# Matmul with batch normalisation: the weight's last two blocks loaded and computed one at a time, the second chunk by halves of rows

## The chip, the cores and the metric

The kernel runs on one core of a Trainium2 chip. The metric is the device time of one execution in microseconds (us), measured without a profiler; the profile beside it is one further execution, recorded. TensorE multiplies, VectorE (DVE), ScalarE (ACT) and GpSimd (POOL) compute, SyncE (SP) and GpSimd issue DMA transfers.

## The reference

```python
# x: (16, 512, 1024), weight: (1024, 768), gamma and beta: (768,), all float32
y = np.matmul(x, weight)
mean = np.mean(y, axis=(0, 1), keepdims=True)
var = np.var(y, axis=(0, 1), keepdims=True)
y_norm = (y - mean) / np.sqrt(var + eps)
return (gamma * y_norm + beta).astype(np.float32)
```

So an 8192 x 1024 matrix is multiplied by a 1024 x 768 one, and each of the 768 columns of the product is normalised by its own mean and variance over all 8192 rows. No output can be written before all 8192 rows of its column are multiplied.

## The kernel before

The 8192 rows are cut into C = 16 chunks of 512 (`CH`), each of two quarters of 256 rows (`QR`); the 1024 inner positions into four blocks (`JW`) of 256; the 768 columns into six groups of 128. x and w are converted to bf16 by the loading DMA. DVE transposes each piece of x into `xT_sb`[...].

Two forms of matmul are used. For column groups 0 and 1 (`GA`) of chunks 0 to 13 the *row form* puts rows of x on the partitions of the result, two blocks of 128 rows in one PSUM bank:

```python
def mm_rows(c, ts, jws, slot):
    def emit(eng):
        if jws[0] == 0:
            y_ps = psum.tile([P, CH], f32, tag="b")
            slot.tile = y_ps
        y_ps = slot.tile.rearrange("p (s n) -> p s n", n=NA)
        for s, t in enumerate(ts):
            for jw in jws:
                for e in range(2):
                    seq(nc.tensor.matmul(
                        y_ps[:, s], x_slot[c].tile[:, jw, t * P:(t + 1) * P, e],
                        w_sb[:, jw, e, 0:NA], ...))
```

For column groups 2 to 5, and for groups 0 and 1 of the last two chunks (`ga_unit`), the *column form* puts the columns on the partitions:

```python
for jw in jws:
    for e in range(2):
        seq(nc.tensor.matmul(
            y_ps, w_sb[:, jw, e, nt * P:(nt + 1) * P],
            x_slot[c].tile[:, jw, q0 * QR:q1 * QR, e], ...))
```

So one row unit is 16 matmuls of 256, one column unit 8 matmuls of 512. Each result bank is read by DVE or ACT for its statistics and copied to bf16 by ACT. There are eight PSUM banks. Row units are squared by ACT, their values added up by DVE and their squares by GpSimd or DVE. After chunk 15 the sums are merged, spread to all partitions by four small matmuls (`a_ps`), and the first outputs are written; the column units of groups 2 to 5 for chunks 4 to 15 fill TensorE's time meanwhile and afterwards.

The kernel is written as tasks with priorities, durations and dependences. A function `arrange` sorts them, as the kernel is built, into one fixed order for each engine[...]. At most eight loads of GpSimd's queue are under way: a load waits for the landing of the load eight before it. One load task issues four DMAs, each for 32 partitions:

```python
def load_w(jw, jw1):
    def emit(eng):
        rows = weight.rearrange("(i jw c e) n -> i c jw (e n)", i=4, jw=JW, e=2)
        dst = w_sb.rearrange("p jw e n -> p jw (e n)")
        for i in range(4):
            seq(nc.gpsimd.dma_start(dst[32 * i:32 * i + 32, jw:jw1], rows[i, :, jw:jw1]))
    return emit

order = [("x", 0), ("w", 0, 1), ("x", 1), ("w", 1, 2), ("w", 2, 4)]
order += [("x", q) for q in range(2, SHORT * QPC)] + [("c", c) for c in range(SHORT, C - 1)]
order += [("p", M - CH, CH - P), ("p", M - P, P)]
```

`("x", q)` is a quarter of x, `("c", c)` a whole chunk, `("p", row, rows)` a part of the last chunk (384 rows, then 128). Chunk 0 is computed as the blocks of w come, chunk 1 by units:

```python
part(0, 1, [0])
...                       # eight idle matmuls that keep TensorE going
part(1, 2, [0])
part(0, 2, [1])
for h in range(2):
    rows_unit(0, [2 * h, 2 * h + 1], [2, 3])
for nt in range(GA, NT):
    col_unit(nt, 0, [2, 3])
...
for c in range(1, RC):
    for ts in ([0, 1], [2, 3]):
        rows_unit(c, ts)
    if c < EARLY:
        for nt in range(GA, NT):
            for jws in halves:
                col_unit(nt, c, jws)
```

Of the kernel before, what the change touches and what calls it, by code (L numbers as in the profile page):

```python
# [227 lines left out]
def kernel(  # L228
# [34 lines left out]
    GY = 2  # L263
    PAD = 36
    HELD = 1
# [60 lines left out]
    msq = singles.tile([P, GA], f32)  # L326
    gst = singles.tile([P, GA, 3 + 12 * (C - RC)], f32)
    seq(nc.vector.memset(gst, float(RC * CH)))
# [20 lines left out]
    def dve(occ):  # L349
        return {"DVE": (occ, occ + 0.09)}  # L350
# [57 lines left out]
    for c in range(C):  # L408
        x_slot[c] = Slot(xts)
    order = [("x", 0), ("w", 0, 1), ("x", 1), ("w", 1, 2), ("w", 2, 4)]  # L410
    order += [("x", q) for q in range(2, SHORT * QPC)] + [("c", c) for c in range(SHORT, C - 1)]
# [3 lines left out]
    for kind, n, *n1 in order:  # L415
# [29 lines left out]
        if rows % QR:  # L445
            t0 = rows // QR * QR // 32
            m1 = m0 + 32 * t0
            c, q = divmod(m1 // QR, QPC)
            x_ready["tile", m1 // P] = task(
                -1000 + t, dve(0.63), turn_x(slot, x_slot[c], m0, t0, 0, JW, False, P),  # L450
                [load, x_ready[c, 0, JW]], uses=[slot, x_slot[c]])
            x_ready[c, q, JW] = x_ready[c, q, JW // 2] = x_ready["tile", m1 // P]
# [3 lines left out]

    def mm_rows(c, ts, jws, slot):
        def emit(eng):
            if jws[0] == 0:
                y_ps = psum.tile([P, CH], f32, tag="b")  # L460
                slot.tile = y_ps
            y_ps = slot.tile.rearrange("p (s n) -> p s n", n=NA)
            for s, t in enumerate(ts):
                for jw in jws:
                    for e in range(2):
                        seq(nc.tensor.matmul(  # L466
                            y_ps[:, s], x_slot[c].tile[:, jw, t * P:(t + 1) * P, e],
                            w_sb[:, jw, e, 0:NA],
                            start=(s == 0 and jw == 0 and e == 0),
                            stop=(jw == JW - 1 and e == 1),  # L470
                            skip_group_check=True,
                        ))
        return emit
# [56 lines left out]

    def rows_unit(c, ts, jws=range(JW)):
        key = "row", c, ts[0]
        slot = bank_of.setdefault(key, None) or Slot(banks)
        bank_of[key] = slot
        kw = {"takes": [slot], "uses": [x_slot[c]]} if jws[0] == 0 else {"uses": [slot, x_slot[c]]}
        h = ts[0] * P // QR
        t = pe_task(0.873 * len(ts) * len(jws) / JW, mm_rows(c, ts, list(jws), slot),
                    waits(jws, c, h, h + 1), key, **kw)
        if jws[-1] == JW - 1:
            rows_stats(c, ts, slot, t)  # L540
        return t
# [21 lines left out]
    def rows_stats(c, ts, slot, t):  # L563
# [11 lines left out]
        def add_rows(eng):  # L575
            seq(nc.vector.tensor_add(sum1, slot.tile[:, 0:n], sum1))  # L576

# [118 lines left out]
    part(0, 2, [1])  # L696
    for h in range(2):
        rows_unit(0, [2 * h, 2 * h + 1], [2, 3])
    for nt in range(GA, NT):
        col_unit(nt, 0, [2, 3])  # L700

# [8 lines left out]

    def more(h):
        def emit(eng):
            seq(nc.gpsimd.tensor_add(tot[:, 1], tot[:, 1], sum3[:, h * NA:(h + 1) * NA]))
        return emit

    ga_half = {}

    def ga_unit(nt, c, q, cols=QR):
        slot = Slot(banks)
        at = 3 + 6 * (2 * (c - RC) + q)  # L720

        def emit(eng):
            y_ps = psum.tile([P, CH], f32, tag="b")
            slot.tile = y_ps
            for jw in range(JW):
                for e in range(2):
                    seq(nc.tensor.matmul(  # L727
                        y_ps[:, 0:cols], w_sb[:, jw, e, nt * P:(nt + 1) * P],
                        x_slot[c].tile[:, jw, q * QR:q * QR + cols, e],
                        start=(jw == 0 and e == 0), stop=(jw == JW - 1 and e == 1),  # L730
                    ))
# [4 lines left out]
        def keep(eng):  # L736
            if "y" not in y_row[c].__dict__:
                y_sb = ypool.tile([P, GA, CH], bf16, tag="y")
                y_row[c].y = y_sb
            seq(nc.scalar.copy(y_row[c].y[:, nt, q * QR:q * QR + cols], slot.tile[:, 0:cols]))  # L740

        t = pe_task(1.808 * cols / CH + 0.01, emit, waits(range(JW), c, q, (q * QR + cols) // QR), takes=[slot],
                    uses=[x_slot[c]])
        late = 40 if c == C - 1 else -3.0
# [3 lines left out]
                 uses=[slot] + ([y_row[c]] if mine else []), takes=[] if mine else [y_row[c]])  # L748
        ga_half[nt, c, q] = b, k

    for c in range(1, RC):
        for ts in ([0, 1], [2, 3]):
# [5 lines left out]
    ends = [row_end[k] for k in row_end]  # L758
    U = clock[0] - 30.0
    for c in range(RC, C):  # L760
        for q in range(QPC):
            for nt in range(GA):
                ga_unit(nt, c, q)
    merges.append(task(U, dve(0.36), merge(0), [k[1] for k in ends], True))
    merges.append(task(U, pool(0.65), merge(1), [k[2] for k in ends]))
    for h in range(2):
        merges.append(task(U, pool(0.65), more(h), merges[1:]))

# [113 lines left out]

    ng = task(S - 30.0, dve(0.1), negate_gamma, [affine], True)

# [309 lines left out]
```

## Time and profile before

| | before |
|---|---|
| time, median of 3 runs | 212.51 us (212.29 to 212.88) |
| span of the profiled execution | 211.0 us |
| busy: TensorE, DVE, ACT, GpSimd | 193.6, 142.4, 127.2, 101.6 us |
| TensorE on the chain that ended last | 82% |
| loaded x and w on GpSimd's queue | 18.36 MB (as bf16) |

The profile divides the span into 40 slices of 5.27 us and shows for each the busy tenths of every engine and of the 16 DMA engines. Matmuls are pipelined and their ends are modelled, so a busy TensorE is not one at its peak; where it starts late after a wait is exact. In a line of a timeline the first number is the start in us from the span's start, the second the duration; `L466` is the line of the program (466: row form, 494: column form, 405: transpose by DVE, 384: load of x, 375: load of w, 727: `ga_unit`), and the bracket at the end tells how long the engine was idle before and what ended that.

### The profile page before, as it was taken

How to read it: one execution, taken by the hardware profiler on the slowest of the kernel's cores; microseconds unless marked ns; L12 is line 12 of the kernel's file. 1: busy time of each engine (PE TensorE's matmuls, PEld its weight loads, DVE VectorE, ACT ScalarE, POOL GpSimd, SP SyncE). 2: the span in 40 equal slices, each digit the busy share in tenths (PEclk: the TensorE clock that was granted, in tenths of full speed). 3: DMA queues.
4: the chain of work that ended last, by engine and by line, in shares of the span. 5: the costliest groups of instructions: out<-in, count | busy, mean ns of one | idle time of the engine just before them, and what ended most of it. 6: DMA issues, size and time to landing. Idle time of an engine off the chain costs nothing.

```text
span 211.0 us, 3457 instructions
## 1 busy us (share of the span) xinstructions
PE 193.6 (92%) x1218; PEld 114.1 (54%) x1234; DVE 142.4 (67%) x233; ACT 127.2 (60%) x233; POOL 101.6 (48%) x126
## 2 busy tenths in 40 slices
PE   7986999999999999999999999999999999996900
PEld 2363564647488888777854544444444455544600
DVE  4220887778759999978979898765963486247800
ACT  2000573435325666758279997999846687955940
POOL 7885967677529999997108985540000000000000
PEclk9999999999999999999999999999999999999985
DMA  5999999999999999999004999998999999994997
GB/s 51 167 179 184 186 196 196 196 197 196 191 193 197 194 198 196 196 196 185 11 2 149 339 385 322 263 355 236 317 253 254 324 322 332 345 347 143 320 347 227
DMA packets 95135, 47.92 MB, mean 227 GB/s; under 512 B 20880, under 2 KB 94608, under 8 KB 95120
## 3 DMA queue, kind: packets, MB, share of 16 engines
q0 software_dynamic: 34688, 18.36, 63.9%
q1 hardware_dynamic: 60432, 29.37, 49.1%
q8 instruction: 9, 0.15, 0.3%
q14 instruction: 6, 0.05, 0.1%
HBM read 36.71 MB, written 25.17 MB: 293 GB/s over the span
## 4 chain that ended last, share of the span: by engine, by line
PE 82%; DMA 6%; ACT 3%; POOL 3%; issue 1%; DVE 1%; ACTq 0%; POOLq 0%
PE y_ps L494 51%; PE y_ps L466 22%; PE y_ps L727 3%; DMA w_sb<-in_weight_dram 3%; ACT o_sb L1143 3%; DMA ring<-in_x_dram 2%; PE o_ps L961 2%; POOL w_sb L375 2%; POOL ring L384 1%; PE y_ps L665 1%; PE o_ps L991 1%; ACTq L1189 0%; PE a_ps L826 0%; PE tot_ps L781 0%; DVE fin L672 0%
## 5 line engine op out<-in xcount | busy, mean ns | idle before, releaser
L494 PE MATMUL y_ps<-xT_sb,w_sb 128*128 128x512 bf16 (+1 forms) x497 | 118.2, 383 | 0.7
L494 PEld LDWEIGHTS <-w_sb 128*128 128x128 bf16 x512 | 48.9, 96 | 62.1
L384 POOL DMA_DIRECT2D ring<-in_x_dram x76 | 47.5, 629 | 14.1 <-DMA ring<-in_x_dram 6.2
L466 PE MATMUL y_ps<-w_sb,xT_sb 128*128 128x256 bf16 x448 | 50.6, 273 | 2.7 <-DMA w_sb<-in_weight_dram 2.2
L466 PEld LDWEIGHTS <-xT_sb 128*128 128x128 bf16 x448 | 43.5, 98 | 10.5 <-issue 2.4
L625 DVE BATCH_NORM_STATS2 stats<-y_ps 128x6 f32<-128x512 f32 x46 | 31.8, 693 | 25.7 <-PE y_ps L494 25.5
L629 ACT CAST y_sb<-y_ps 128x512 bf16<-128x512 f32 x51 | 29.5, 586 | 26.0 <-DVE stats L625 17.6
L405 DVE STREAM_TRANSPOSE xT_sb<-ring 128x1024 f32<-128x1024 f32 (+1 forms) x35 | 38.2, 1128 | 10.2 <-DMA ring<-in_x_dram 10.2
L573 ACT ACTIVATE sq_sb<-y_ps 128x512 f32<-128x512 f32 x28 | 16.1, 598 | 27.3 <-PE y_ps L466 26.1
L859 POOL TENSOR_TENSOR ring<-ring,sum 128x1024 f32<-128x1024 f32 (+1 forms) x11 | 22.7, 2091 | 17.5 <-ACT sum L830 10.2
L580 POOL TENSOR_TENSOR sum<-sum,sq_sb 128x512 f32<-128x512 f32 x18 | 23.0, 1280 | 7.1 <-ACT sq_sb L573 6.6
L576 DVE TENSOR_TENSOR sum<-y_ps,sum 128x512 f32<-128x512 f32 x28 | 18.9, 676 | 10.7 <-ACT sq_sb L573 9.6
L586 ACT CAST y_sb<-y_ps 128x512 bf16<-128x512 f32 x28 | 16.2, 585 | 10.0 <-DVE sum L576 9.9
L961 PE MATMUL o_ps<-ident,y_sb 128*128 128x128 bf16 x128 | 17.1, 220 | 1.8 <-DVE y_sb L1130 1.6
L854 DVE TENSOR_TENSOR ring<-y_sb,a_ps 128x1024 f32<-128x1024 bf16 (+1 forms) x16 | 16.7, 1078 | 1.5 <-PE a_ps L826 0.8
L1057 ACT CAST ring<-ring 128x1024 f32<-128x1024 bf16 x16 | 16.7, 1048 | 0.8 <-DMA ring<-y_sb 0.8
L510 PE MATMUL idle_ps<-idle_sb 128*128 128x512 bf16 x37 | 10.8, 460 | 1.2 <-DVE idle_sb L309 1.2
L961 PEld LDWEIGHTS <-y_sb 128*128 128x128 bf16 x128 | 9.3, 97 | 3.8 <-DVE y_sb L1130 2.0
L940 ACT ACTIVATE y_sb<-y_sb,shift,scale 128x1024 bf16<-128x1024 bf16 x8 | 9.8, 1244 | 0.0
L634 ACT ACTIVATE y_sb<-y_ps 128x512 bf16<-128x512 f32 x12 | 7.1, 594 | 3.8 <-PE y_ps L494 3.8
L1035 ACT CAST ring<-o_ps 128x1024 f32<-128x1024 bf16 x8 | 8.1, 1024 | 0.3 <-DMA out_dram<-ring 0.3
L510 PEld LDWEIGHTS <-idle_sb 128*128 128x128 bf16 x38 | 4.2, 114 | 7.1 <-issue 3.3
(87 smaller groups left out, 113.1 us busy)
## 6 DMA issues: line engine op xcount, KB each, us to landing
out_dram<-ring SPq DMA_DIRECT2D x38, 512.0 KB, 3.9
ring<-in_x_dram POOLq DMA_DIRECT2D x52, 256.0 KB, 9.1
out_dram<-o_sb SPq DMA_DIRECT2D x6, 512.0 KB, 5.2
ring<-in_x_dram POOLq DMA_DIRECT2D x16, 128.0 KB, 5.4
out_dram<-ring SPq DMA_DIRECT2D x4, 256.0 KB, 2.1
w_sb<-in_weight_dram POOLq DMA_DIRECT2D x8, 96.0 KB, 4.8
w_sb<-in_weight_dram POOLq DMA_DIRECT2D x4, 192.0 KB, 6.3
ring<-in_x_dram POOLq DMA_DIRECT2D x4, 192.0 KB, 8.0
```

The source lines that it names most:

```text
L384: seq(nc.gpsimd.dma_start(x_bf[32 * i:32 * i + 32], src[:, :, KQ * i:KQ * (i + 1)]))
L405: seq(nc.vector.transpose(dst, src[:, :, jw0:jw1]))
L466: seq(nc.tensor.matmul(y_ps[:, s], x_slot[c].tile[:, jw, t * P:(t + 1) * P, e], w_sb[:, jw, e, 0:NA], start=(s == 0 and jw == 0 and e == 0 ...
L494: seq(nc.tensor.matmul(y_ps, w_sb[:, jw, e, nt * P:(nt + 1) * P], x_slot[c].tile[:, jw, q0 * QR:q1 * QR, e], start=(jw == 0 and e == 0 and ...
L576: seq(nc.vector.tensor_add(sum1, slot.tile[:, 0:n], sum1))
L580: seq(ENG[eng].tensor_add(acc, acc, state["sq"][:, 0:n]))
L625: seq(nc.vector.bn_stats(dst, slot.tile))
L629: seq(nc.scalar.copy(y(nt, c), slot.tile))
L854: seq(nc.vector.tensor_mul(slot.o, y_row[c].y[:, s0:s1], aff[0][:, None, :].to_broadcast([P, n, NA])))
L859: seq(ENG[eng].tensor_add(slot.o, slot.o, row[:, None, :].to_broadcast([P, n, NA])))
L961: seq(nc.tensor.transpose(dst, src, ident))
L1057: seq(nc.scalar.copy(slot.o, t_slot.o))
```

## The change

The change is to the order of work, not to what is computed. It is for starting block 2 of w as soon as it is there, and for not needing the second half of a chunk's rows at once.

- Blocks 2 and 3 of w are two load tasks of four 96 KB DMAs instead of one of four 192 KB, and chunk 0 is computed with block 2 first for all its units, then with block 3.
- Chunk 1 is computed for its first 256 rows (row unit, then four column units of 256), then for the others.
- The last chunk's column form of groups 0 and 1 is cut into 256, 128 and 128 rows instead of 256 and 256, so that only the last piece needs the last load of x.
- The merging of the sums of squares (GpSimd) has a later priority, and the negation of gamma waits for the diagonal matrix of the scale, so that it stands later in DVE's order.

The functions `mm_rows` and `rows_unit` get an argument `part` that is not used with any value but the whole; the statistics' storage gets one entry more per group.

```diff
-    order = [("x", 0), ("w", 0, 1), ("x", 1), ("w", 1, 2), ("w", 2, 4)]
+    order = [("x", 0), ("w", 0, 1), ("x", 1), ("w", 1, 2), ("w", 2, 3), ("w", 3, 4)]
...
-    for h in range(2):
-        rows_unit(0, [2 * h, 2 * h + 1], [2, 3])
-    for nt in range(GA, NT):
-        col_unit(nt, 0, [2, 3])
+    for jw in (2, 3):
+        for h in range(2):
+            rows_unit(0, [2 * h, 2 * h + 1], [jw])
+        for nt in range(GA, NT):
+            col_unit(nt, 0, [jw])
...
-    for c in range(1, RC):
+    rows_unit(1, [0, 1])
+    for nt in range(GA, NT):
+        col_unit(nt, 1, range(JW), 0, 1)
+    rows_unit(1, [2, 3])
+    for nt in range(GA, NT):
+        col_unit(nt, 1, range(JW), 1, 2)
+    for c in range(2, RC):
...
-        for q in range(QPC):
+        for r0, cols in ((0, QR), (QR, QR)) if c < C - 1 else ((0, QR), (QR, P), (QR + P, P)):
             for nt in range(GA):
-                ga_unit(nt, c, q)
+                ga_unit(nt, c, at, r0, cols)
+            at += 6
...
-    merges.append(task(U, pool(0.65), merge(1), [k[2] for k in ends]))
+    merges.append(task(U + 34, pool(0.65), merge(1), [k[2] for k in ends]))
     for h in range(2):
-        merges.append(task(U, pool(0.65), more(h), merges[1:]))
+        merges.append(task(U + 34, pool(0.65), more(1, sum3, h), merges[1:]))
...
-    ng = task(S - 30.0, dve(0.1), negate_gamma, [affine], True)
+    ng = task(S, dve(0.1), negate_gamma, [affine, dg], True)
```

Since the order of every engine is made anew by `arrange`, instructions far from these lines move too.

## The prediction

> **What bounds the kernel now.** I read three views in this order: the slices of the page, the waits of TensorE, and the timeline of the first 30 us and of 74 to 100 us.
>
> The page's busy tenths and transfer rate in 40 slices (5.27 us each):
>
> ```profile
> PE   7986999999999999999999999999999999996900
> DMA  5999999999999999999004999998999999994997
> GB/s 51 167 179 184 186 196 196 196 197 196 191 193 197 194 198 196 196 196 185 11 2 149 339 385 322 263 355 236 317 253 254 324 322 332 345 347 143 320 347 227
> ```
>
> TensorE is full from the fifth slice to the 36th. The only loose places are the first four slices (21 us) and the last four. The DMA engines are full too while x is loaded, up to slice 19 (100 us), at about 195 GB/s counted on the bf16 side. Loads stop there; stores then run at up to 385 GB/s, and in slice 37, just before the tail, at only 143: no backlog of stores stands in front of the tail.
>
> The stretches view gives the same with PE's busy time, its clock, the DMA share and the rate at the end of each line, and the TensorE waits are few (total us, times, longest):
>
> ```profile
> 20.30:58.00 37.70, 37.43 (x222) 21.72 (x227) 30.16 (x40) 17.62 (x31) 26.67 (x37) 1.00 1.48 194
> 58.00:98.20 40.20, 40.07 (x343) 33.46 (x343) 34.71 (x44) 24.82 (x48) 34.03 (x43) 1.00 1.47 196
> ...
> PE y_ps L466 <- DMA w_sb<-in_weight_dram: 2.2, 2, 1.9
> PE o_ps L961 <- DVE y_sb L1130: 1.6, 1, 1.6
> PE idle_ps L510 <- DVE idle_sb L309: 1.2, 1, 1.2
> PE y_ps L466 <- DVE xT_sb L405: 0.5, 1, 0.5
> ```
>
> From 20.30 to 192.6 us TensorE never waits for more than a few hundredths. So what is saved before 20.30 moves everything behind it, and the largest single wait there is the 1.9 us for w. The timeline shows it (start, duration, engine, line, operation):
>
> ```profile
> 16.42 1.97 PE L494 MATMUL y_ps<-xT_sb,w_sb 128*128 128x512 bf16 x8
> 16.81 0.57 POOL L384 DMA_DIRECT2D ring<-in_x_dram  x1 [0.39 <-DMA w_sb<-in_weight_dram]
> 18.59 0.57 POOL L384 DMA_DIRECT2D ring<-in_x_dram  x1 [1.21 <-DMA w_sb<-in_weight_dram]
> 19.51 0.57 POOL L384 DMA_DIRECT2D ring<-in_x_dram  x1 [0.35 <-DMA w_sb<-in_weight_dram]
> 20.30 1.91 PE L466 MATMUL y_ps<-w_sb,xT_sb 128*128 128x256 bf16 x16 [1.91 <-DMA w_sb<-in_weight_dram]
> 22.61 0.68 DVE L580 TENSOR_TENSOR sum<-sum,sq_sb 128x512 f32<-128x512 f32 x1
> 23.21 1.24 DVE L405 STREAM_TRANSPOSE xT_sb<-ring 128x1024 f32<-128x1024 f32 x1
> 25.66 3.68 PE L466 MATMUL y_ps<-w_sb,xT_sb 128*128 128x256 bf16 x32
> 26.15 1.22 DVE L405 STREAM_TRANSPOSE xT_sb<-ring 128x1024 f32<-128x1024 f32 x1
> ```
>
> TensorE ends block 1 of w on chunk 0 at 18.39 and starts blocks 2 and 3 at 20.30. The four 192 KB pieces that carry both blocks landed one by one: each GpSimd load at 16.81, 18.59 and 19.51 was released by the landing of one (about 16.5, 18.3, 19.2), and the fourth ended TensorE's wait at 20.2. Blocks 2 and 3 of chunk 0 then take 20.30 to 25.66 = 5.36 us, and chunk 1 follows without a gap.
>
> **What the Trainium skill says.** *TensorE: Matmul & The Clock Gate*, section "Wait — 56ns, not 53.3ns?", gives a warm matmul N cycles plus a fixed 2.5 ns. By it, cutting a 512-wide matmul into two of 256 costs 2.5 ns (estimate). The trace agrees: eight 512-wide in 1.81 us are 226 ns each; the 16 of 256 at L665 take 1.83 us, 114 ns each, two for 229 ns. *The same page*, Part 1, says the clock falls after an idle window of about 3.4 us; TensorE's idle time here is at most 1.91 us and the granted clock stays 1.00 to 192.6 us, so removing the idle time buys no clock. *DMA: Bandwidth & Descriptors*, "Anatomy of one DMA", puts a fixed cost of about 2 us on each load, mostly the wait for the completion; that can lie beside other transfers as long as enough of them are under way. The trace agrees on the second half: the rate stays at 179 to 186 GB/s in slices 3 to 5 with 96 KB and 192 KB pieces mixed.
>
> **The change part by part.**
>
> *1. Blocks 2 and 3 apart.* Eight loads of 96 KB replace four of 192 KB; same bytes, 4 more issues on GpSimd of 0.53 us (from the chain, L375). The built program shows x's third quarter issued after them, as before. Block 1 landed at about 15.3 (the landing records), both later blocks by 20.2. Half the bytes should land about midway, 17 to 18 us (estimate from these two). TensorE wants block 2 at 18.3, so that wait goes. Block 2 of chunk 0 is 8 row matmuls of 256 at 0.109 = 0.87 us and 8 column matmuls of 512 at 0.226 = 1.81 us, together 2.68 us. Block 3 is wanted at 18.3 + 2.7 = 21.0 and is there by 20.2. Chunk 0 ends at 18.3 + 5.36 = 23.7 instead of 25.66: **-1.95 us** on the path.
>
> *2. Second chunk by halves.* Before, chunk 1 wanted rows 0-255 at 25.66 (transpose done 24.45) and rows 256-511 at 27.41 (done 27.37): the second with nothing to spare. Moved 1.95 us earlier, the old order would wait for it. In the new order TensorE does rows 0-255 for the row block (1.75 us) and for four column blocks (32 matmuls of 256 at 114 ns = 3.65 us), so the second half is wanted 5.4 us after the start. The new wait is the first half. Its last piece landed at 22.88 by the landing records; the DVE transpose takes 1.24 us, so chunk 1 can start at about 24.2, not 23.7: **+0.5 us**. (The squares' addition at 22.61 that stood before this transpose is no longer there in the new order.) The second half is transposed by about 27, wanted at 29.6: no wait. Chunk 2 is wanted at 35.0, and its two transposes ended at 33.56. Cutting costs 32 more matmuls x 2.5 ns = **+0.08 us**.
>
> *3. From chunk 4 to 13* TensorE gains on the loads. Before, chunk 11's first transpose ended at 81.95 and its matmuls started about 82.5; chunks 12 and 13:
>
> ```profile
> 85.75 2.37 DVE L405 STREAM_TRANSPOSE xT_sb<-ring 128x1024 f32<-128x1024 f32 x2
> 91.25 2.36 DVE L405 STREAM_TRANSPOSE xT_sb<-ring 128x1024 f32<-128x1024 f32 x2
> ...
> 87.60 3.66 PE L466 MATMUL y_ps<-w_sb,xT_sb 128*128 128x256 bf16 x32
> 92.90 3.65 PE L466 MATMUL y_ps<-w_sb,xT_sb 128*128 128x256 bf16 x32
> ```
>
> The first of each pair is done at 86.99 and 92.49, 0.4 to 0.6 us before use. Loads cannot come earlier, the DMA engines being full. TensorE must fill the gained 1.4 us with work that needs no new x. The new program's order does that: a half column unit of 0.905 us now stands ahead of chunk 11, and by the first units of chunk 14 one more half unit has been done than before. Adding up on TensorE from 24.2: chunk 11 at 81.9 against 81.95, chunk 12 at 87.2 against 86.99, chunk 13 at 92.5 against 92.49, chunk 14 at 97.8 against 97.98. I allow **+0.2 us** for these edges.
>
> *4. Last chunk in three pieces.* The last 256 rows become twice 128: 16 more small matmuls, +0.04 us, and two more statistics and copies, on DVE and ACT. The last quarter's transposes ended at 102.65 and 103.25; before, TensorE reached that quarter at about 104.5, and will reach it at about 104.2. No wait was there to remove; the piece matters only as insurance.
>
> *5. Negation later, squares' sums later on GpSimd.* The negation stood in DVE's order waiting 3.7 us for gamma (56.9 to 60.64). DVE then had slack: TensorE had no wait near it. **0 us**. The two small matmuls that spread scale and shift move one or two half units back in the order; the first stores then start about 0.5 us later, with 143 GB/s before the tail showing room.
>
> Sum: -1.95 + 0.5 + 0.08 + 0.2 + 0.04 = -1.1 us; 212.5 - 1.1 = 211.4. As the third quarter may land a little sooner (its pieces no longer compete with 192 KB ones), I take **211.3 us**.
>
> **The rivals.**
> - *The landing does not move.* Pieces of one queue overlap: of the old four, the first landed 3.7 us before the last. If the two blocks' pieces interleave, block 2 lands at 19 and the gain is 1.2 at the head, 0.6 in the end: 211.9. Against it: earlier blocks of 96 KB pieces landed at about 0.5 us a piece.
> - *x becomes the bound.* The DMA engines were full to 100 us, and chunks 11 to 14 had 0.4 to 0.6 us to spare. If the loads slip by half a microsecond (more issues on GpSimd, whose sums now stand in long runs between loads), TensorE waits at each edge and the gain is eaten: 212.3. Against: column units are at hand as fillers.
> - *The later stages give it back.* TensorE's order has transposes that stand between matmuls and wait for ACT's normalisation; ACT is busy for 90% or more of slices 22 to 24 and 26 to 28. If the first such blocks come 1 us sooner than ACT can, the wait returns there: 212.2.
> - *Everything works*, x's quarter lands at 22.3: the full 1.95 less 0.2: 210.7.
>
> **Range and chances.** The ceiling is the removed idle time of 1.9 us (210.5); the floor is a gain eaten by new waits, and a reordered program can lose some tenths. Range 210.5 to 212.3. Two per cent is 4.25 us, over twice all the idle time concerned, so within 2% is nearly certain.
>
> **What would show it.** Right: TensorE's wait for w near 18 us gone or under 0.3; its chunk 1 starting at 24.0 to 24.4 after a transpose; the rest of the chain moved rigidly; the tail after TensorE's last column unit still 18.4 us. Wrong: a wait of 0.5 us or more for a transpose between 77 and 100 us, matmuls interleaved with transposes waiting for ACT after 110 us, or a new wait for w at 18 us.

## The result, and the profile after

| | before | changed |
|---|---|---|
| time, median | 212.69 us (212.29 to 213.0) | 215.58 us (215.31 to 216.38) |
| ratio | | 1.0143 (95%: 1.0111 to 1.0176) |
| span of the profile | 211.0 us | 214.3 us |
| TensorE starts its last column unit at | 190.62 us | 192.26 us |
| from there to the end | 20.37 us | 22.03 us |

The change costs 2.9 us; the prediction said 211.3 us. The profile puts the loss in two places of about the same size: TensorE gets to its last column unit 1.64 us later, and what follows takes 1.66 us longer.

The page after the change, busy tenths and rate in 40 slices (of 5.36 us now):

```profile
PE   7989799999999998999999999999999999996700
GB/s 62 158 191 123 180 196 194 197 196 196 194 190 196 197 196 196 197 196 182 14 0 132 231 355 310 258 374 321 232 278 270 282 328 343 259 336 347 343 347 153
```

TensorE has a 9 in slice 4 where there was a 6, as hoped, but a 7 in slice 5 and an 8 in slice 16. The rate falls to 123 GB/s in slice 4 (16 to 21 us; 184 before). The two slices before the last are both full (343, 347), and the last one moves 153 GB/s where before it moved 227.

TensorE's waits after (total us, times, longest), and its stretches (PE's busy time is the second number). Line numbers have moved with the change: L469 is now the row form, L497 the column form, L738 `ga_unit`; L583 and L587 are DVE's additions to the sums.

```profile
PE y_ps L469 <- DVE xT_sb L405: 3.7, 4, 1.5
PE o_ps L979 <- DVE y_sb L1148: 1.6, 1, 1.6
...
0.00:20.30 20.30, 18.05 (x89) 9.30 (x91) 4.76 (x13) 1.49 (x2) 17.19 (x37) 1.00 0.94 134
20.30:58.00 37.70, 36.04 (x245) 23.72 (x247) 29.13 (x39) 17.06 (x30) 26.64 (x37) 1.00 1.45 191
58.00:98.20 40.20, 38.91 (x334) 32.38 (x334) 32.70 (x41) 24.54 (x48) 34.32 (x44) 1.00 1.48 196
```

The wait for w is gone; in its place stand 3.7 us of waits for transposed x. Up to 20.30 us TensorE did 1.7 us more work (18.05 us against 16.34). From there to 98.2 us, where it was idle for 0.4 us before (37.70 - 37.43 and 40.20 - 40.07), it is idle for 2.95 us: 2.55 us given back for 1.7 won.

The chain that ended last, by line, before and then after:

```profile
by line: PE y_ps L494 51.4%; PE y_ps L466 22.4%; PE y_ps L727 3.4%; DMA w_sb<-in_weight_dram 3.1%; ACT o_sb L1143 2.9%; DMA ring<-in_x_dram 2.5%; PE o_ps L961 2.2%; POOL w_sb L375 1.7%; issue 1.5%; POOL ring L384 1.2%; PE y_ps L665 0.9%; PE
by line: PE y_ps L497 37.8%; DMA ring<-in_x_dram 22.0%; issue 5.4%; POOL ring L384 4.4%; DVE xT_sb L405 3.6%; PE y_ps L738 3.4%; PE y_ps L469 3.3%; ACT o_sb L1161 2.9%; PE o_ps L979 2.1%; DVE sum L583 1.9%; POOL sum L587 1.8%; POOL w_sb L37
```

Before, the chain left the transfers at 20.30 us and was TensorE's own. Now transfers of x are 22% of it and their issue on GpSimd 4.4%: x has become the bound up to 100 us.

How it begins, first on GpSimd before (issues of w, L375, and of x, L384), then on GpSimd, TensorE and DVE after:

```profile
13.59 0.53 POOL L375 DMA_DIRECT2D w_sb<-in_weight_dram  x1 [0.26 <-DMA ring<-in_x_dram]
14.14 2.28 POOL L384 DMA_DIRECT2D ring<-in_x_dram  x4
...
13.91 2.42 POOL L375 DMA_DIRECT2D w_sb<-in_weight_dram  x5 [0.82 <-DMA ring<-in_x_dram]
16.32 4.00 POOL L384 DMA_DIRECT2D ring<-in_x_dram  x7
...
18.56 1.03 PE L469 MATMUL y_ps<-w_sb,xT_sb 128*128 128x256 bf16 x8
21.24 1.04 PE L469 MATMUL y_ps<-w_sb,xT_sb 128*128 128x256 bf16 x8
25.55 1.70 PE L469 MATMUL y_ps<-w_sb,xT_sb 128*128 128x256 bf16 x14 [1.47 <-DVE xT_sb L405]
...
24.25 1.25 DVE L405 STREAM_TRANSPOSE xT_sb<-ring 128x1024 f32<-128x1024 f32 x1 [1.05 <-DMA ring<-in_x_dram]
```

Blocks 2 and 3 run on without a gap (18.56, 21.24). But the fourth piece of block 2 had to wait for x's second quarter to land (13.9 us), and four more issues, 2 us, follow before x's third quarter can be issued: at 16.32 us, where before it was 14.14. By the landing records it lands at 24.13 instead of 22.88 us and is transposed from 24.25, so chunk 1 starts at 25.55 instead of 25.66: 0.1 us is left of the 1.95. From chunk 2 on, loads come at a steady 5.35 us a chunk, so most of the lag stays: chunk 2 lands at 33.31 instead of 31.06 us, the last piece of x at 103.19 instead of 101.57. That is 1.62 us, as much as TensorE's last column unit is late.

Two things hold that issue at the same time. GpSimd is busy with the issues of w until 16.32 us; and the load eight before it, which must have landed first, is now the first piece of block 2 (15.97 us by the landing records), where it was the first piece of block 1 (13.85; the issue followed 0.29 us later). So quicker issues of the same loads would not have brought x's issue back to 14.14 us.

From chunk 9 to 12 there is a second thing, on DVE:

```profile
70.95 0.69 DVE L583 TENSOR_TENSOR sum<-y_ps,sum 128x512 f32<-128x512 f32 x1 [0.75 <-ACT sq_sb L579]
71.55 2.36 DVE L405 STREAM_TRANSPOSE xT_sb<-ring 128x1024 f32<-128x1024 f32 x2
73.84 1.45 DVE L583 TENSOR_TENSOR sum<-y_ps,sum 128x512 f32<-128x512 f32 x2
75.20 0.68 DVE L587 TENSOR_TENSOR sum<-sum,sq_sb 128x512 f32<-128x512 f32 x1
76.63 0.69 DVE L583 TENSOR_TENSOR sum<-y_ps,sum 128x512 f32<-128x512 f32 x1 [0.74 <-ACT sq_sb L579]
77.24 2.36 DVE L405 STREAM_TRANSPOSE xT_sb<-ring 128x1024 f32<-128x1024 f32 x2
```

The next chunk's transposes (77.24) stand behind an addition that waits 0.74 us for ACT's squares of the unit just computed. The loop takes 77.24 - 71.55 = 5.69 us a chunk, more than the loads' 5.35. TensorE's later waits, 1.2 us in two times, lie here.

The tail in 40 parts, from the start of the last column unit to the end, GB/s; first before (190.6 to 211 us), then after (192.2 to 214.3 us) with its instruction queue:

```profile
GB/s 350 345 246 25 21 5 0 0 0 100 349 349 342 346 342 342 349 345 346 351 340 350 346 345 349 343 350 346 345 348 344 348 344 349 345 346 144 0 0 0
...
GB/s 349 345 347 350 344 347 348 343 351 344 347 350 362 320 334 340 343 347 348 344 352 344 345 350 343 349 348 344 351 346 346 347 346 349 153 21 19 0 0 0
q8 instruction: 1, 0.02, 0.3%
```

Both tails are stores at some 346 GB/s. Before, they end at once. After, two parts of 0.55 us follow at 21 and 19 GB/s: a sixteenth of 346, one DMA engine alone, 1.1 us behind the other fifteen. In the 14th to 16th part the rate had dipped to 320 to 340, and in this tail lies one packet of the queue "instruction", of 16 KB. By the packet records it comes at 199.1 us and takes 1.04 us. Before, no such packet lies in the tail: the last two come at 182.9 us and at 212.7, past the end. The other 0.5 us of the longer tail is open. Backlog suggests itself, as 6.6 MB were left to store when the last column unit began and 5.2 MB before; but of the runs below e3 has a tail of 22.00 us with 4.8 MB left, and e13 one of 20.37 us with 5.9 MB.

### The profile page after: what moved, and what is told of

It reads as the page before. It is cut to its first block, busy times and chain, and to the rows that moved or that the text cites. A ratio compares the mean times of both kernels' runs of the same rounds, so it can differ in the third digit from the quotient of the medians.

```text
span 214.3 us, 3558 instructions
## 1 busy us (share of the span) xinstructions
PE 194.9 (91%) x1267; PEld 118.9 (55%) x1282; DVE 141.3 (66%) x234; ACT 126.9 (59%) x235; POOL 104.8 (49%) x131
## 4 chain that ended last, share of the span: by engine, by line
PE 49%; DMA 22%; POOL 7%; DVE 6%; issue 5%; ACT 5%; ACTq 0%; DVEq 0%; POOLq 0%
PE y_ps L497 38%; DMA ring<-in_x_dram 22%; POOL ring L384 4%; DVE xT_sb L405 4%; PE y_ps L738 3%; PE y_ps L469 3%; ACT o_sb L1161 3%; PE o_ps L979 2%; DVE sum L583 2%; POOL sum L587 2%; POOL w_sb L375 1%; PE y_ps L672 1%; ACT sq_sb L579 1%; ACT y_sb L593 1%; PE o_ps L1009 0%
## 5 line engine op out<-in xcount | busy, mean ns | idle before, releaser
L497 PE MATMUL y_ps<-xT_sb,w_sb 128*128 128x512 bf16 (+1 forms) x530 | 118.3, 370 | 0.7
L497 PEld LDWEIGHTS <-w_sb 128*128 128x128 bf16 x544 | 51.9, 96 | 58.9
L384 POOL DMA_DIRECT2D ring<-in_x_dram x76 | 47.4, 629 | 16.8 <-DMA ring<-in_x_dram 5.7
L469 PE MATMUL y_ps<-w_sb,xT_sb 128*128 128x256 bf16 x448 | 51.1, 273 | 3.7 <-DVE xT_sb L405 3.7
L469 PEld LDWEIGHTS <-xT_sb 128*128 128x128 bf16 x448 | 43.5, 98 | 11.9 <-DVE xT_sb L405 5.5
L632 DVE BATCH_NORM_STATS2 stats<-y_ps 128x6 f32<-128x512 f32 x46 | 30.8, 688 | 20.7 <-PE y_ps L497 20.6
L583 DVE TENSOR_TENSOR sum<-y_ps,sum 128x512 f32<-128x512 f32 x28 | 18.9, 674 | 11.8 <-ACT sq_sb L579 11.0
L587 POOL TENSOR_TENSOR sum<-sum,sq_sb 128x512 f32<-128x512 f32 x19 | 24.3, 1280 | 2.8 <-ACT sq_sb L579 1.8
L979 PE MATMUL o_ps<-ident,y_sb 128*128 128x128 bf16 x128 | 17.7, 242 | 1.8 <-DVE y_sb L1148 1.6
L979 PEld LDWEIGHTS <-y_sb 128*128 128x128 bf16 x128 | 10.7, 110 | 3.1 <-DVE y_sb L1148 2.0
L375 POOL DMA_DIRECT2D w_sb<-in_weight_dram x16 | 7.9, 496 | 1.2 <-DMA ring<-in_x_dram 0.8
```

The source lines that it names most:

```text
L384: seq(nc.gpsimd.dma_start(x_bf[32 * i:32 * i + 32], src[:, :, KQ * i:KQ * (i + 1)]))
L469: seq(nc.tensor.matmul(y_ps[:, s], x_slot[c].tile[:, jw, t * P:(t + 1) * P, e], w_sb[:, jw, e, 0:NA], start=(s == 0 and jw == 0 and e == 0 ...
L497: seq(nc.tensor.matmul(y_ps, w_sb[:, jw, e, nt * P:(nt + 1) * P], x_slot[c].tile[:, jw, q0 * QR:q1 * QR, e], start=(jw == 0 and e == 0 and ...
L583: seq(nc.vector.tensor_add(acc, slot.tile[:, 0:n], acc))
L587: seq(ENG[eng].tensor_add(acc, acc, state["sq"][:, 0:n]))
L632: seq(nc.vector.bn_stats(dst, slot.tile))
```

## The experiments: which part of the change costs

Theory at this point: the four additional issues make x late, and that is the loss. Rivals: small pieces leave too few bytes under way; or the new orders on TensorE and DVE cost the time. "Last unit" is the start of TensorE's last column unit, "tail" from there to the end.

**e1, the split of the load alone, in the kernel before.** Every engine's order of computation is kept but for one addition of squares that goes from DVE to GpSimd.

```diff
-    order = [..., ("w", 1, 2), ("w", 2, 4)]
+    order = [..., ("w", 1, 2), ("w", 2, 3), ("w", 3, 4)]
```

> The kernel before with only the load of w's blocks 2 and 3 cut into two tasks of four 96 KB pieces; TensorE's order is exactly that of before, DVE's differs by one addition that moves to GpSimd. Theory A (smaller pieces leave too few bytes under way, the load queue runs dry near 20 us and every later load is late): x's third quarter lands at about 24.1 instead of 22.9 us, chunk 2 at about 33 instead of 31, the last load at about 103 instead of 101.6, and the time is 1 to 3 us longer than before. Theory B (the new order of the computation delays things, the loads only follow): loads land as before, time within 0.5 us of before.

Measured: 215.33 us against 212.76, ratio 1.0124 (1.0072 to 1.0177). The timeline of GpSimd, and TensorE's waits:

```profile
13.62 2.41 POOL L375 DMA_DIRECT2D w_sb<-in_weight_dram  x5 [0.21 <-issue]
16.03 4.59 POOL L384 DMA_DIRECT2D ring<-in_x_dram  x8
...
28.41 1.92 PE L466 MATMUL y_ps<-w_sb,xT_sb 128*128 128x256 bf16 x16 [1.09 <-DVE xT_sb L405]
```

x is issued at 16.03 us and its last piece lands at 102.64; last unit 191.60 (+0.98), tail 21.60. The split alone makes x and TensorE late, in the old order. Of the 2.6 us, 1.2 are its longer tail, which holds a packet, too.

**e2, the change without the split.**

```diff
-    order = [..., ("w", 2, 3), ("w", 3, 4)]
+    order = [..., ("w", 2, 4)]
```

> The changed kernel with blocks 2 and 3 of w loaded as before in four 192 KB pieces; all other parts of the change stay (block-wise chunk 0, chunk 1 by halves, last chunk in three, merges and negation later). Theory A: loads land as before (third quarter 22.9, chunk 2 at 31), time 212 to 213 us. Theory B: about as long as the changed kernel, 215 us or more.

Measured: 213.70 us, 1.0040 (1.0022 to 1.0058). x is issued at 13.69 us, last unit 189.26, tail 21.91. Of the change's 2.9 us, undoing the split takes back 1.9. What is left is in the tail: TensorE's end is not late.

**e3 and e4, chunk 1 in four pieces of 256 KB instead of eight of 128 KB**, in the changed kernel and in the one before: more bytes under way.

```diff
-    SHORT = 2
+    SHORT = 1
```

> The changed kernel with chunk 1 of x loaded in four 256 KB pieces instead of eight of 128 KB, so that 0.4 + 1 MB are under way near 18 us. Theory A: the queue does not run dry, chunk 1 is all there by about 25 to 26 us and chunk 2 by about 31, the end of loads as before; TensorE waits at chunk 1 until about 26.5, then no later waits for x; time 212 to 213.5 us. Theory B: chunk 1 starts later than in the changed kernel (25.55 us), so the time is 215.5 us or more.

> The kernel before with chunk 1 of x loaded in four 256 KB pieces. Theory A: more bytes under way remove the dip of the rate near 24 us (155 instead of 195 KB per us), the loads end 0.2 to 0.5 us earlier; chunk 1 starts later at about 26.5 us since it needs the whole chunk; time within 1 us of before. Theory B says the same of the loads' place: no change, and 1 us longer for the later start.

Measured: e3 220.91 us, 1.0385 (1.0337 to 1.0432); e4 216.60 us, 1.0184 (1.0136 to 1.0232). e3's rate still falls in slice 4, with x issued at 16.31 us:

```profile
GB/s 56 175 174 121 192 196 196 196 197 196 187 192 196 183 167 187 173 173 172 39 0 97 297 378 372 234 321 263 254 303 321 327 327 310 347 347 45 332 347 146
```

Larger pieces behind the same late issue don't fill the gap, so too few bytes is not what makes the dip. In both, chunk 1 is now wanted whole: TensorE waits 4.9 us for it in e3, 2.0 us in e4.

**e9, lateness alone.** In the kernel before, two additions of zeros on GpSimd ahead of x's third quarter (2.17 us by the trace); loads, pieces and orders are untouched.

```diff
     def emit(eng):
+        if m0 == CH:
+            for _ in range(2):
+                seq(nc.gpsimd.tensor_add(sum2, sum2, sum2))
```

> The kernel before with all its loads as they were, but two additions of zeros (1.28 us each) on GpSimd ahead of the issue of x's third quarter, so that it is issued at about 16.7 instead of 14.14 us; all orders are those of before. Theory C (what counts is how long before the end of w's transfers the next x is issued: in the changed kernel four more issues stand before it, 16.3 instead of 14.1 us, and x needs 3 to 4 us from its issue to a full stream): the rate dips at 19 to 21 us, the third quarter lands at 24 instead of 22.9, chunk 2 at about 32.3 instead of 31.1, the last load about 1.2 us later, time 1.5 to 3 us longer. Theory A (smaller pieces as such): no dip, times of before within 0.5 us.

Measured: 214.90 us against 213.02, 1.0108 (1.0075 to 1.0141). (Two of e9's thirteen runs, and one each of e19's and e21's six, were of a slower state that executions here can fall into, and the medians leave them out.) Its timeline, and a stretch of TensorE with the granted clock as the third number from the end:

```profile
13.61 2.17 POOL L384 TENSOR_TENSOR sum<-sum 128x512 f32<-128x512 f32 x2
15.73 5.21 POOL L387 DMA_DIRECT2D ring<-in_x_dram  x9
...
28.57 3.48 PE L469 MATMUL y_ps<-w_sb,xT_sb 128*128 128x256 bf16 x16 [2.19 <-DVE xT_sb L408]
...
20.00:58.00 38.00, 35.55 (x203) 20.52 (x205) 28.46 (x38) 16.66 (x29) 24.62 (x34) 0.96 1.42 188
```

An issue at 15.73 us is enough to make TensorE wait 2.19 us for x's fourth quarter (landed at 27.14 instead of 25.76; the third was in time at 22.21) and to cost 1.9 us, with a tail of 20.36 us. So two additions ahead of the issue, with nothing else changed in the program, cost about as much as the split. But e9 does not repeat what the changed kernel does:

- Its profile is of an execution of 216.36 us. There only 1.4 us of the lag stood at chunk 2 (32.48 us); the last piece came 3.8 us late, at 105.33. Its loads ran at 173 to 186 GB/s in slices 11 to 15, where the changed kernel's run at 190 to 197.
- After the wait of 2.19 us its granted clock was at half for 3.41 us (from 28.72 us, by the clock's records), hence the 0.96. That is up to 1.7 us of TensorE's time (estimate: half of 3.41), and neither the changed kernel nor e1 has it. It is not the whole loss: e9's four runs with a mean clock of 0.984 or 0.985, where the highest of the kernel before is 0.986, still took 213.70 to 215.11 us.

**e5, x's third quarter between the blocks.**

```diff
-    order = [..., ("w", 2, 3), ("w", 3, 4)] + [("x", 2), ("x", 3)] + ...
+    order = [..., ("w", 2, 3), ("x", 2), ("w", 3, 4), ("x", 3)] + ...
```

> The changed kernel with x's third quarter loaded between w's blocks 2 and 3 (w2, x, w3, x). Theory C: x is issued at about 13.9 us again, the queue does not run dry, the last load lands at 101 to 102 as before; block 3 lands at about 22 and chunk 1 starts at about 24.8 instead of 25.66 us; time 212 to 213.5 us. Theory A (the small pieces themselves): still a dip and 215 us.

Measured: 216.47 us, 1.0162 (1.0132 to 1.0191). The third quarter was issued at 13.25 us and landed at 20.56, the fourth at 25.21; but TensorE waited 2.4 us for block 3, chunk 2 landed at 32.55 instead of 31.06 and the last piece at 103.12. The lateness was moved one chunk on, not removed; and the clock was at half for 3.41 us after that wait, as in e9.

**e6, chunk 1 by halves alone**, and **e8, the later merge and negation alone**, in the kernel before.

```diff
+    rows_unit(1, [0, 1])
+    for nt in range(GA, NT):
+        col_unit(nt, 1, range(JW), 0, 1)
+    rows_unit(1, [2, 3])
+    for nt in range(GA, NT):
+        col_unit(nt, 1, range(JW), 1, 2)
-    for c in range(1, RC):
+    for c in range(2, RC):
```

> The kernel before with chunk 1 alone computed by halves of rows. 32 more matmuls at 2.5 ns; no wait to save, since w sets the start. All theories: loads as before, time within 0.4 us of before.

```diff
-    merges.append(task(U, pool(0.65), merge(1), ...))          # and the two after it
+    merges.append(task(U + 34, pool(0.65), merge(1), ...))
-    ng = task(S - 30.0, dve(0.1), negate_gamma, [affine], True)
+    ng = task(S, dve(0.1), negate_gamma, [affine, dg], True)
```

> The kernel before with the merges of squares and the negation of gamma later, only DVE's order moves, by that one instruction. If DVE's wait of 3.7 us for gamma cost nothing: within 0.4 us of before. If it held back transposes and with them the issue of loads (chunk 7 of x was transposed 2.7 us after its landing): up to 1 us shorter.

Measured: e6 214.80 us, 1.0077 (1.0049 to 1.0104); e8 213.17 us, 1.0005 (0.9989 to 1.0022). e8 shows step 5 of the prediction right. e6 was a riddle: its loads (last piece 101.63 us) and last unit (190.76 us) were those of the kernel before, yet it cost 1.7 us. Its tail showed where:

```profile
GB/s 348 348 346 347 346 347 349 198 0 274 348 347 345 363 322 334 337 347 346 347 348 346 347 348 346 347 347 346 348 347 346 348 345 348 119 21 19 0 0 0
...
q8 instruction: 1, 0.02, 0.3%
```

Stores even pause (0 GB/s in the ninth part), so backlog is not it; but the 21 and 19 are there again, and the packet (at 198.1 us). All kernels up to here fall in two groups: tail 20.4 us and no packet in it (before, e4, e8, e9), tail 21.6 to 22.0 us and a packet in it (after, e1, e2, e3, e5, e6).

## The experiments: the packet in the tail

The traces have 1234 weight loads of TensorE before, 1266 in e6 and 1282 after the change, and a matmul was added with each: 64 and 96 instructions more. Between two packets lie 218 to 277 of TensorE's recorded instructions before the change, 253 on average. The page *Runtime: NRT & Kernel Launch* of the Trainium skill agrees ("Instruction fetch mechanics": each engine's instructions are refilled in blocks of 16 KiB, 256 instructions) and calls the cost mostly hidden. If this is the cause, a few more instructions at the start, with no work, must move the packet and the time with it. The idle matmuls at the start are the place: cut in pieces, they have the same columns and more instructions.

```diff
-    seq(nc.tensor.matmul(idle_ps, idle_sb[:, 0:P], idle_sb, ...))
+    for a, b in ((0, 256), (256, 512)):                    # e10: 76 instructions more
+    for a, b in ((0, 256), (256, 384), (384, 512)):        # e12, e13, e14: 152 more
+        seq(nc.tensor.matmul(idle_ps[:, a:b], idle_sb[:, 0:P], idle_sb[:, a:b], ...))
```

> The kernel before; each idle matmul 128x512 of the wake and of the fill is made as two of 128x256 (38 more matmuls with their 38 weight loads, 76 TensorE instructions; same columns, nothing else moves). Fetch theory (the end grows because a 16 KB packet of TensorE's instructions, which comes about every 256 instructions, falls among the last stores): the last packet, in the kernel before outside the tail (182.9 us and 212.7 us), falls at about 197 us, the time from the first matmul of the last column unit to the end grows from 20.4 to about 21.6 us, TensorE gets to that unit at 190.6 us as before, and the time is 213.7 to 214.4 us with the kernel before at 212.8. Order theory (the longer end of the changed kernel comes from its order of tasks and its store backlog): end 20.4 us, time as before within 0.2%.

> The changed kernel with w's last two blocks in one load (213.7 us), and each idle matmul 128x512 made as three of 256, 128 and 128 columns (76 more matmuls, 152 TensorE instructions; same columns). Fetch theory: the packet that fell at 196.0 us, inside the tail, falls at about 186 us, ahead of it; the tail is 20.4 us again instead of 21.9 and the time 212.0 to 212.6 us, a little under the kernel before. Order theory: tail 21.9 us, time 213.7 us.

> The changed kernel, with the idle matmuls in three pieces each (152 more TensorE instructions). Fetch theory: the packet at 199.1 us falls at about 189 us, the tail is 20.4 instead of 22.0 us and the time 214.0 to 214.5 us: what the late loads cost alone, 1.3 to 1.6 us over the kernel before. Order theory: tail 22.0 us, time 215.6 us.

> The kernel before with the second chunk by halves of rows alone (214.8 us; its loads and its last column unit came as in the kernel before, and only its tail was 1.3 us longer), with the idle matmuls in three pieces each. Fetch theory: the packet at 198.1 us falls at about 188 us, the tail is 20.4 us and the time that of the kernel before within 0.3%. Order theory: tail 21.6 us, time 214.8 us.

| | base | time, us | with more idle matmuls, us | ratio to before | tail, us | packet at, us |
|---|---|---|---|---|---|---|
| e10 | before | 212.71 | 213.71 | 1.0066 (1.0041 to 1.0091) | 21.79 | 196.8 |
| e12 | e2 | 213.70 | 212.56 | 0.9992 (0.9971 to 1.0013) | 20.36 | 183.5 |
| e13 | changed | 215.58 | 214.65 | 1.0121 (1.0075 to 1.0168) | 20.37 | 183.7 |
| e14 | e6 | 214.80 | 212.85 | 1.0001 (0.9979 to 1.0023) | 20.35 | 185.5 |

The tails of e10 (189.4 to 211.3 us), and of e13 (191.7 to 212.2 us):

```profile
GB/s 348 187 22 22 5 0 0 0 0 283 347 346 343 363 323 333 337 348 344 347 348 344 350 349 344 346 349 344 351 344 347 347 344 346 42 22 19 0 0 0
q8 instruction: 1, 0.02, 0.3%
...
GB/s 347 345 349 348 345 349 344 6 0 75 346 349 346 343 348 341 350 345 346 349 346 348 348 347 348 345 348 348 345 348 350 342 349 349 342 349 126 0 0 0
```

The packet is put into the kernel before and its tail grows by 1.4 us; it is taken out of three others and their tails shrink to 20.4. In a tail of stores the fetch is thus not hidden. This part is shown. The times follow it: the ratio to the kernel before rises by 0.7% in e10, and falls by 0.5% from e2 to e12 and by 0.8% from e6 to e14. From the changed kernel to e13 it falls by 0.2% only, which their intervals (1.0111 to 1.0176 and 1.0075 to 1.0168) don't separate. The lone sixteenth fits what the page *DMA: Bandwidth & Descriptors* says in "Queues, rings and completion order": every DMA engine takes the queues it has work for in turn, a whole packet at a time. While all sixteen have stores to do, the engine that carries the instructions would be behind by that much, and the last store would wait for it.

With this out of the way the rest is plain: e14, halves alone, costs nothing; e12, everything but the split, costs nothing and gains nothing; e13, everything, costs 1.2%. So the split costs 1.9 us by the medians (2.6 by the ratio, 1.6 to 3.6), and all the other parts together are worth zero within 0.3%.

Two cautions. A single profile does not tell this cost, since when x comes also differs from one execution to the next: the last piece of x lands at 100.61 us in e10's profile and at 102.25 in e12's, and neither has the split. And e12 and e13 differ in DVE's order, too. A transpose in e12 and then one in e13:

```profile
80.88 2.37 DVE L405 STREAM_TRANSPOSE xT_sb<-ring 128x1024 f32<-128x1024 f32 x2 [0.20 <-DMA ring<-in_x_dram]
...
82.43 2.36 DVE L405 STREAM_TRANSPOSE xT_sb<-ring 128x1024 f32<-128x1024 f32 x2
```

The chunk had landed at 80.76 us in e12 and at 81.25 in e13: e12's transposes follow the landings at once, 5.35 us apart, while e13 has the loop of 5.69 us and with it 1.15 us of TensorE's waits. The loop is not needed for a loss, as e1 (5.05 us a chunk) and e5 (5.35) don't have it and their last units are 0.98 and 1.26 us late; but a share of e13's 1.9 us may be its own.

## The experiments: taking the lateness away

To show that the issues do it, they must be taken away with the split kept. Six kernels tried; each changed something else as well.

**e15, e17, e18: single blocks by two issues for 64 partitions each** (e15: blocks 2 and 3 of e13; e18: all four blocks of e13; e17: blocks 0 and 1 of the kernel before).

```diff
-    for i in range(4):
-        seq(nc.gpsimd.dma_start(dst[32 * i:32 * i + 32, jw:jw1], rows[i, :, jw:jw1]))
+    for i in range(0, 4, 2):
+        seq(nc.gpsimd.dma_start(dst[32 * i:32 * (i + 2), jw:jw1], rows[i:i + 2, :, jw:jw1]))
```

> The changed kernel with the idle matmuls in three pieces (214.65 us), and w's blocks 2 and 3 loaded by two issues of 192 KB each instead of four of 96 KB, so that GpSimd makes no more issues before x than in the kernel before. Late-issue theory: x's third quarter is issued at about 14.3 us instead of 16.3 and lands at about 22.9, the last piece of x lands at 101.6 instead of 102.7, the time is 212.4 to 213.2 us, about that of the kernel before; the removed wait for w gives nothing, because TensorE's last column unit starts 89.0 us (88.6 to 89.2) after the last piece of x has landed, as it did in nine of the kernels before this one. Rival (the split itself, or VectorE's new order with its 5.69 us loop, costs the time): 214.2 us or more. Rival (the removed wait is worth its 1.9 us once x is in time): 210.5 to 211.5 us.

> The kernel before with w's blocks 0 and 1 loaded by two issues of 192 KB each instead of four of 96 KB: four issues of about 0.5 us fewer on GpSimd ahead of x. Late-issue theory, turned round: x's third quarter is issued up to 2 us earlier (about 12.2 us); the loads can gain only what the transfer rate lost in the first slices (about 1.5 us at the full rate of 196 GB/s), so the last piece lands at 100.5 to 101.4 us and the time is 211.7 to 212.7 us. Rival (bytes, not issues, bound the head by now, or the first block's larger pieces land later): last piece at 101.6 us or later, 212.7 to 213.5 us.

> As e15, with w's blocks 0 and 1 by two issues each as well: four issues fewer than the kernel before. Late-issue theory: last piece of x at 100.5 to 101.4 us, the last column unit 89.0 us later, 211.5 to 212.7 us. Rival (bytes bound the head): as e15 within 0.3 us.

Measured: e15 219.14 us, 1.0305 (1.0269 to 1.0341); e17 217.89 us, 1.0262 (1.0230 to 1.0294); e18 222.81 us, 1.0484 (1.0458 to 1.0511). All are far slower than any time that was named. e15's page and GpSimd's timeline:

```profile
GB/s 50 176 139 140 107 130 197 196 196 197 196 191 194 197 197 197 195 196 196 112 3 2 193 332 385 298 347 329 246 265 285 273 310 340 332 271 335 289 347 231
DMA packets 96928, 47.95 MB, mean 220 GB/s; under 512 B 22672, under 2 KB 96400, under 8 KB 96912
...
24.33 6.73 POOL L386 DMA_DIRECT2D ring<-in_x_dram  x11 [7.35 <-DMA w_sb<-in_weight_dram]
```

There are 22,672 packets under 512 B; the kernel before has 20,880. In the packet records the new ones have 4 bytes and lie among the pieces of w, which move at about half their usual rate; a 192 KB piece takes 11.8 us from issue to landing (median; 6.3 in the kernel before), and GpSimd stands 7.35 us for one of them. So these three measure a slow form of load, not the number of issues. The attempt failed.

**e19: blocks 1 and 2 in one load of the usual form, block 3 alone** (on e13), and **e20: blocks 1 to 3 in one load** (on the kernel before). As many issues ahead of x as before, and four fewer.

```diff
-    order = [..., ("w", 1, 2), ("w", 2, 3), ("w", 3, 4)]
+    order = [..., ("w", 1, 3), ("w", 3, 4)]          # e19
-    order = [..., ("w", 1, 2), ("w", 2, 4)]
+    order = [..., ("w", 1, 4)]                       # e20
```

> The changed kernel with the idle matmuls in three pieces (214.65 us), with w's blocks 1 and 2 in one load of four pieces of 192 KB and block 3 alone in four of 96 KB: as many issues ahead of x as in the kernel before, in the forms that both kernels have. TensorE's order is the same until chunk 12. Late-issue theory: x's third quarter is issued at about 14.1 us instead of 16.3, lands at about 22.9, the last piece of x at 101.4 to 101.9 instead of 102.7, TensorE waits about 2 us for block 1 instead and this costs nothing, because its last column unit starts 88.6 to 89.2 us after the last piece of x; time 212.3 to 213.2 us. Rival (TensorE's order and VectorE's 5.69 us loop cost the time): 214.2 us or more. Rival (the wait for w is what costs): 214.5 us or more, with the last piece of x at 101.6.

> The kernel before with w's blocks 1 to 3 in one load of four pieces of 288 KB: four issues fewer ahead of x. Late-issue theory: x's third quarter is issued at about 12 us; the last piece of x lands at 100.5 to 101.5 us; TensorE waits for block 1 until about 20 us, some 3 to 4 us more than in the kernel before. If a wait in the head is free as long as x is the bound, the time is 211.7 to 212.8 us; if TensorE has no such room, it is 213.5 to 215.5 us, as in e4, where TensorE stood for the second chunk and lost 1.8%.

Measured: e19 215.74 us against 212.97, 1.0122 (1.0079 to 1.0165); e20 219.51 us, 1.0340 (1.0287 to 1.0393). In e19 the issue at 14.03 us and the landing at 22.33 came as wanted, and the time did not fall. Three of chunk 2's four pieces were in time (29.61 us; 29.74 before); the fourth landed at 32.30, with an instruction packet at 30.2 in between. The last piece of x came at 101.97 us, 0.4 us late, so most of e19's loss lies behind it: the wait for w was back (2.2 us), TensorE's order differs from chunk 4 on, and the last unit began 90.0 us after the last piece of x, where it is 88.6 to 89.1 us in thirteen of the twenty profiles, the kernel before, the changed one and e12 among them. In e20 TensorE waited 3.8 us for block 1, its clock was at half for 3.41 us, and it lost 6.5 us; the head has no such room.

**e21: block 3 off GpSimd** (on e13): loaded in fp32 by SyncE into a buffer of xT that is free, when x's second quarter is transposed, and converted by ScalarE.

```diff
-    order = [..., ("w", 2, 3), ("w", 3, 4)]
+    order = [..., ("w", 2, 3)]
+    gate = task(-990, dve(0.1), open_w3, [x_ready[0, 1, JW // 2]], takes=[w3_slot])   # one memset
+    got = task(2.0, {"SP": (2.0, 2.0)}, load_w3, [gate], dma=..., uses=[w3_slot])
+    w_ready[JW - 1] = task(2.0, act(1.5), cast_w3, [got], uses=[w3_slot])
```

> The changed kernel with the idle matmuls in three pieces (214.65 us); w's block 3 is loaded in fp32 by SyncE, held back until x's first half chunk is transposed (about 14.5 us), into a buffer of xT that is free then, and converted to bf16 by one ScalarE copy 128x1536 (estimate 1.5 us from its 128x512 copies of about 0.5 us). GpSimd has four issues fewer ahead of x. Late-issue theory: x's third quarter is issued at about 14 us instead of 16.3, chunk 2 lands at 31 to 31.5 us and the last piece of x at 101.3 to 101.9; block 3 is ready at about 21.5 us, TensorE waits for it under 1 us; time 212.3 to 213.3 us. Rival (what made the split cost is elsewhere: TensorE's or VectorE's order): 214.2 us or more with the last piece of x at 101.9 us or before. Third outcome (SyncE's transfers take the place in the wires, and x is late all the same): last piece at 102.5 us or later, 214 us or more.

Measured: 218.61 us against 212.43, 1.0221 (1.0158 to 1.0285): the third outcome. ACT's timeline, TensorE's wait, and a stretch of TensorE:

```profile
24.96 1.47 ACT L470 CAST w_sb<-w_f 128x1536 bf16<-128x1536 f32 x1 [22.73 <-DMA w_f<-in_weight_dram]
...
PE y_ps L489 <- ACT w_sb L470: 5.0, 1, 5.0
...
20.00:58.00 38.00, 32.83 (x220) 22.06 (x221) 25.66 (x35) 16.76 (x28) 23.42 (x33) 0.91 1.42 197
```

x was issued at 14.45 us, but SyncE's transfers, issued from 15.16 us, ran at the same time: its third quarter landed at 25.21, block 3 at 24.9, and TensorE stood for 5.0 us. Then its granted clock fell too, to 0.91 of full speed in this stretch (1.00 in e13). *TensorE: Matmul & The Clock Gate*, Part 1, has the clock fall after an idle window of about 3.4 us, which fits here; but in e9 and e5 waits of 2.19 and 2.35 us sufficed, so the page's figure is not the least that does it.

So it stays open how much of the split's cost is the late issue alone. Shown are: the split costs 1.3 to 2.1 us by the medians, when put in (e1, without its longer tail) and when taken out (e12 against e13); with the two blocks apart the last piece of x is late (102.64 us in e1, 102.72 in e13, 103.12 in e5, 103.19 after; 101.57 before), and TensorE's last unit follows it by 88.8 to 89.1 us in these five; and late issue without the split costs 1.9 us, but in part by other ways (e9). Not shown is a kernel with the split, x in time and the time back. No version was faster than the kernel before.

## Why the prediction was wrong

*Step 1, the wait for w.* The mechanism was right: block 2 landed at 17.46 us (17 to 18 predicted) and TensorE ran on at 18.56. What failed is the conclusion from TensorE's never waiting after 20.30 us, "so what is saved before 20.30 moves everything behind it". A chain without waits says that TensorE is full, not that x has slack. Everything but the split still has waits for w (1.7 us in e12), and e13 has 0.3 us of them; e13 is the slower by 2.1 us.

*Step 2, chunk 1's start*, is the term that was mis-sized. It took the third quarter's landing, 22.88 us, from the old trace. Measured 24.13, and chunk 1 at 25.55 instead of 24.0 to 24.4: +1.85 us for the +0.5 of the sum. The four issues stood in step 1, counted at 0.53 us each, and were not put on x's path, though x's issue comes right behind them and, with eight loads under way, had to wait for a landing four pieces later (15.97 instead of 13.85 us). The text even expected the quarter "a little sooner".

*Step 3, chunks 11 to 14*, +0.2 us, failed by size: TensorE's idle time from 58 to 98.2 us went from 0.13 to 1.29 us, as the loads were 1.6 us later and DVE's loop took 5.69 us. How much that loop costs beside the loads was not isolated.

*The costs of cutting* (steps 2 and 4) are too small to be seen: e14, with the first, is 1.0001, and e12, with both, 0.9992. *Step 5* was right (e8).

*"The tail still 18.4 us"* failed. The instructions that the change adds were counted as TensorE time, 0.12 us, never as instructions to be fetched. They moved a fetch into the stores: the tail is 1.66 us longer in the profile, and as short as before in e13 (20.37 us), where 152 idle instructions move the fetch out again; by the medians that is worth 0.9 us, which the intervals of the two don't separate.

*The rivals.* "x becomes the bound", with the issues on GpSimd as the reason, came nearest, but was capped at a gain eaten (212.3 us). Late transfers have no such cap: without the packet the changed kernel takes 214.65 us. The range left out that a change meant to save could cost.

## What to carry to other kernels

When a load is cut into more pieces, follow the queue's next load, not only the one that was cut. Each further piece ahead of it puts its issue time on it, and where the number of loads under way is limited, also makes it wait for a later landing. Where transfers are the bound to the end of loading, as here, little of that is given back. Before believing a gain or loss of half a per cent in a kernel that ends in stores, look for an instruction packet in the tail; moving it by some idle instructions tells whether the change did anything else. And where an experiment makes TensorE wait, look at its granted clock before the loss is put down to the wait alone.

## What the runs showed of the hardware

- One 16 KB fetch of TensorE's instructions, 0.95 to 1.11 us on one of sixteen DMA engines, among stores that fill all sixteen goes with an end that is 1.2 to 1.4 us longer (e1, e6, e10), 0.6 to 0.7% of this kernel. A tail can take it on by very little: e1 has TensorE's order of the kernel before, with one more wait for a semaphore (31 against 30 in the traces), and its packet came at 204.4 us instead of past the end. Only three of TensorE's instructions start after 200 us in the kernel before.
- TensorE's granted clock fell to half for 3.41 us after waits of 2.19 us (e9) and 2.35 us (e5), and for 6.83 us after waits of 4.90 us (e3) and 5.04 us (e21). After one of 2.20 us in e19 it did not.
- A load whose source has two levels behind its 64 partitions adds packets of 4 bytes and lands in 11.8 us instead of 6.3 (e15).
- One ScalarE conversion 128x1536 from fp32 to bf16 takes 1.47 us (e21).
